# TensorE's order in two attention stages, laid out by the kernel itself

## The chip, the cores and the metric

The kernel runs on one core of a Trainium2 chip. The metric is the device time of one execution in microseconds (us). The kernel before took 3550.54 us, the median of three runs (3549.37 to 3552.87). A core has five engines that matter here, each with a queue of its own that it works through in order: TensorE (PE in the profile: matmuls and transposes), VectorE (DVE), ScalarE (ACT), GpSimd (POOL) and SyncE (SP), which here issues the DMAs. They wait for each other by semaphores.

## The reference

The program computes two layers of a hybrid block over 512 tokens of width 1024, and then one second block. Only two of the four branches of the second block change. Both are attention over 16 heads of 64, and both start from the normed input `h`:

```python
fq = _rms(_heads(proj("fox_q"), FOX_HEADS), fox_q_norm_g[l])
fk = _rms(_heads(proj("fox_k"), FOX_HEADS), fox_k_norm_g[l])
log_f = jax.nn.log_sigmoid(proj("fox_f") + b_forget[l])
# fox, per block of 128 queries
logits = einsum('bhqd,bhkd->bhqk', qi, k) * scale + (fi - cum_f)
p = softmax(where(k_pos <= q_pos, logits, -inf));  y = p @ v
# stick-breaking, per block of 128 queries
z = einsum('bhqd,bhkd->bhqk', qi, k) * scale
log_1m_beta = where(causal, log_sigmoid(-z), 0.0)
excl = cumsum(log_1m_beta, axis=3, reverse=True) - log_1m_beta
weights = where(causal, exp(log_sigmoid(z) + excl), 0.0);  y = weights @ v
# all four branches
gates = sigmoid(proj("gates") + b_gate[l])
mixed = sum(gates * einsum('bsnc,ncd->bsnd', branches, w_branch[l]), axis=2)
```

## The kernel before

All data stay transposed in SBUF, with features on the partitions and the 512 tokens along the free axis. A product in single precision is made of three matmuls with operands split into a high and a low part (`mm3`, L308 to L310: high by high, high by low, low by high). Weights come by DMA as `raw`; ScalarE makes the high part (L293), GpSimd or VectorE the low part (L296, in turns).

The second block runs its branches one behind the other: mem, fox, lru, sb (stick-breaking). In fox and sb the heads go in pairs p, since two heads of 64 fill the 128 partitions. The steps are

- `Q`p and `K`p: a projection of 24 matmuls of 128x512 into a bank `pd`. In fox the norm of K follows (`knorm`): sums by head on TensorE into the bank `pm`, a reciprocal root on GpSimd, a copy on VectorE (L860), a broadcast by four transposes (L864), a product on VectorE (L895). Then `halves` splits K on ScalarE (L427) and GpSimd (L429), and `stack_k` copies the halves by four DMAs of SP (L449) into the tiles `qk` and `e`. Q goes the same way by `stack_q` (L440).
- `V`g: values of four heads, 96 matmuls of 128x256 into `pd`.
- `H`h: one head. Four rows of logits (128 queries by 128, 256, 384 and 512 keys) by two matmuls each into `pa` (L456). In fox each row then gets its bias (made on GpSimd, L1014 and L1016), its minimum on VectorE (L473), the exponential on ScalarE, the reciprocal on VectorE (L479) and the normalisation on GpSimd (L480). In sb each row goes through two sigmoids on ScalarE (L495, L496), two selects on GpSimd (L498), a scan on VectorE (L501) and a multiply on GpSimd (L502). Then `weigh` transposes the weights by ten transposes into `pt` (L514), ScalarE and VectorE split them (L302, L303), eight matmuls sum the values into `po` (L523), and `fold` brings `po` out (VectorE, L532). The second head of a pair ends with `ys`, the pair's output, split by L302.
- `G`d: one of the eight gates of the branch, 24 matmuls into `pd`, a product on VectorE (L910) and a DMA to memory.

Behind the heads `branch` multiplies the `ys` with the branch's weights in the bank `pa`, 24 matmuls for each of eight tiles.

The kernel calls these steps in the order of two written plans, `FOX_PLAN` (L34) and `SB_PLAN` (L36), through `run` (L950). That is the program's order, not yet the engines' order: a scheduler at build time, with a timing model of its own, then chooses for every engine the order of its instructions, within the data's dependencies. In the trace heads, projections and gates therefore stand mixed. Banks bound what can overlap: two `pd`, two `pa` (three in sb, with `pm`), two `pt`, one `po`, one `pm`.

Of the kernel before, what the change touches and what calls it, by code (L numbers as in the profile page):

```python
# [10 lines left out]
def _warn_once_fixed(msg, *args, **kwargs):  # L11
# [6 lines left out]
FT = mybir.dt.float32  # L18
# [4 lines left out]
P = 128  # L23
# [173 lines left out]

class Build:
    def __init__(self, ctx, tc, I):
        self.tc, self.nc, self.I = tc, tc.nc, I  # L200
        nc = self.nc
# [104 lines left out]
    def mm3(self, out, wh, wl, xh, xl, start, stop):  # L306
        mm = self.nc.tensor.matmul
# [33 lines left out]
    def rstd_of(self, acc, d):  # L341
        nc = self.nc
        pt = self.ps("pm")
        for t in range(4):
            nc.tensor.matmul(pt[:, t:t + 1], acc[:, t * P:(t + 1) * P], self.ones[:, 0:1], start=True, stop=True)
# [3 lines left out]
        for t in range(4):  # L349
            nc.tensor.transpose(pt[:, t * P:(t + 1) * P], y[:, t:t + 1].to_broadcast([P, P]), self.ident)  # L350
# [102 lines left out]
    def dots(self, ps, q, k, s, t, n):  # L453

        for x in range(2):
            self.nc.tensor.matmul(ps[:, :n], q[:, s, t], k[s][:, x, :n], start=x == 0, stop=x == 1)  # L456

    def head(self, q, k, rows, bias, v, sub, y, tmp=None, scale=None):


        nc = self.nc
        st, po = self.sp.tile([P, 1280], FT, name="st"), self.ps("po")
        for i in range(4):
            n = (i + 1) * P
            c = slice(OFF[i], OFF[i] + n)
            ps = self.logits()
            t = slice(i * P, (i + 1) * P)
            if rows is None:
                self.dots(ps, q, k, sub, t, n)
            else:  # L470
                self.mm3(ps[:, :n], q[rows, 0, t], q[rows, 1, t], k[rows, 0, :n], k[rows, 1, :n], True, True)
            mn, sm = self.tiny(1, "ta"), self.tiny(1, "ta")
            nc.vector.tensor_tensor_reduce(st[:, c], ps[:, :n], bias(i), -1.0, 3e38, OP.add, OP.min, mn)  # L473
            f = -1.0
            if scale is not None:
                f = scale(i)
                nc.vector.tensor_scalar(mn, mn, f, -1.0, op0=OP.mult, op1=OP.mult)
            nc.scalar.activation(st[:, c], st[:, c], AF.Exp, bias=mn, scale=f, accum_out=sm)
            nc.vector.reciprocal(sm, sm)  # L479
            nc.gpsimd.tensor_scalar(st[:, c], st[:, c], sm, 0.0, op0=OP.mult, op1=OP.add)  # L480
        self.weigh(st, v, sub, po)
        self.fold(po, y, tmp)

    def stick(self, q, k, v, sub, y, tmp):

        nc = self.nc
        st, po = self.sp.tile([P, 1280], FT, name="st"), self.ps("po")
        for i in range(4):
            n = (i + 1) * P
            ps = self.logits()  # L490
            t = slice(i * P, (i + 1) * P)
            self.dots(ps, q, k, sub, t, n)
            r = self.f()
            o = OFF[i]
            nc.scalar.activation(r[:, :n], ps[:, :n], AF.Sigmoid, scale=-1.0)  # L495
            nc.scalar.activation(st[:, o:o + n], ps[:, :n], AF.Sigmoid)  # L496
            for d, fill in ((r[:, t], 1.0), (st[:, o + n - P:o + n], 0.0)):
                nc.gpsimd.affine_select(out=d, in_=d, pattern=[[-1, P]], compare_op=OP.is_gt, fill=fill, base=0,  # L498
                                        channel_multiplier=1)
            b = r[:, :n][:, ::-1]  # L500
            nc.vector.tensor_tensor_scan(b, b, b, 1.0, op0=OP.mult, op1=OP.min)  # L501
            nc.gpsimd.tensor_mul(st[:, o:o + n - 1], st[:, o:o + n - 1], r[:, 1:n])  # L502
        self.weigh(st, v, sub, po)
        self.fold(po, y, tmp)

    def weigh(self, st, v, sub, po):

        nc = self.nc
        va = v.rearrange("p a b -> p (a b)")
        for js in ((0,), (1,), (2, 3)):  # L510
            pt, at, cols = self.ps("pt"), 0, []
            for j in js:
                for i in range(j, 4):
                    nc.tensor.transpose(pt[:, at + (i - j) * P:at + (i - j + 1) * P],  # L514
                                        st[:, OFF[i] + j * P:OFF[i] + (j + 1) * P], self.ident)
                cols.append((j, at))
                at += S - j * P
            w = self.hl("pt")
            self.split(w, pt[:, :at], cols=slice(0, at))
            for j, c in cols:  # L520
                o = j * 256 + sub * P
                for x in range(2):
                    nc.tensor.matmul(po[:, j * P:], va[:, o:o + P], w[:, x, c:c + S - j * P], start=j == 0 and x == 0,  # L523
                                     stop=j == 3 and x == 1)
# [819 lines left out]
```

## Time and profile before

| | |
|---|---|
| median of three runs | 3550.54 us (3549.37 to 3552.87) |
| the profiled execution | 3547.29 us, span 3545.5 us, granted clock 0.99 |
| TensorE busy | 3450.4 us, 97% of the span, 16,392 instructions |
| VectorE, ScalarE, GpSimd busy | 55%, 40%, 43% |
| DMA | 397.57 MB, 112 GB/s |
| fox, 2350 to 2600 us | TensorE idle 13.9 us, of which 11.4 behind 2540 |
| sb, 2860 to 3106 us | TensorE idle 9.8 us, of which 4.6 behind 3060 |

Idle time of TensorE is the length of a window less the first number of busy time in its row. PEclk is the share of the full clock (2.4 GHz) that was granted to TensorE; at 0.5 it runs at 1.2 GHz. In a timeline a number in brackets is how long the engine stood idle ahead of the row, and behind it what released it.

### The profile page before, as it was taken

The numbers are of one execution on the slowest core, as the hardware profiler recorded it, in microseconds if no ns is written. First come the engines' busy times: TensorE is split into PE (matmuls) and PEld (weight loads), VectorE is DVE, ScalarE is ACT, GpSimd is POOL, SyncE is SP. The second block draws the span as 40 slices with busy tenths as digits, with TensorE's granted clock in tenths as the row PEclk, the third lists the DMA queues.
The fourth block names the chain that finished last, engine by engine and source line by source line (L and its number), as shares of the span: only waits on it lengthen the run. The fifth ranks groups of instructions, "written<-read, shape, count | busy, mean of one in ns | idle before, by whom it ended". The sixth has DMA issues, their size and how long they took to land.

```text
span 3545.5 us, 44868 instructions
## 1 busy us (share of the span) xinstructions
PE 3450.4 (97%) x16392; PEld 2864.3 (81%) x16392; DVE 1967.6 (55%) x3210; ACT 1435.7 (40%) x2366; POOL 1536.4 (43%) x1224
## 2 busy tenths in 40 slices
PE   8999999999999999999999999999999999999999
PEld 7888777788888888777888888888777788888887
DVE  5434697653445344796643456348646656657363
ACT  4223455532233223465432245346635445533222
POOL 3333346342424242446333344248545567635342
PEclk9999999999999999999999999999999999999999
DMA  4233433323233334334323233244532454442332
GB/s 135 92 104 106 129 94 110 115 95 95 99 97 96 93 98 130 109 91 118 117 90 109 85 124 119 97 137 141 151 122 89 164 154 137 120 143 96 95 101 89
DMA packets 141259, 397.57 MB, mean 112 GB/s; under 512 B 18144, under 2 KB 21600, under 8 KB 141040
## 3 DMA queue, kind: packets, MB, share of 16 engines
q1 hardware_dynamic: 141040, 394.71, 36.1%
q8 instruction: 130, 2.13, 0.2%
q14 instruction: 89, 0.73, 0.1%
HBM read 327.24 MB, written 20.48 MB: 98 GB/s over the span
## 4 chain that ended last, share of the span: by engine, by line
PE 47%; DVE 5%; ACT 2%; POOL 2%; issue 2%; DMA 1%; SPq 0%; POOLq 0%; DVEq 0%; ACTq 0%
PE pd L308 10%; PE pd L309 10%; PE pd L310 10%; PE pa L308 4%; PE pa L309 4%; PE pa L310 4%; PE po L523 1%; PE pt L514 1%; PE pa L456 1%; DVE wl L296 1%; DVE st L1083 0%; ACT wh L293 0%; POOL st L502 0%; DVE x L658 0%; DVE t L657 0%
## 5 line engine op out<-in xcount | busy, mean ns | idle before, releaser
L296 POOL TENSOR_TENSOR wl<-raw,wh 128x1024 fp32r<-128x1024 f32 (+3 forms) x315 | 719.6, 2285 | 1130.9 <-ACT wh L293 1122.2
L293 ACT ACTIVATE wh<-raw 128x1024 fp32r<-128x1024 f32 (+3 forms) x631 | 609.6, 967 | 1322.7 <-PE pd L309 841.9
L308 PE MATMUL pd<-hs,wh 128*128 128x512 f32 (+1 forms) x2008 | 792.4, 395 | 21.3 <-ACT wh L293 7.4
L310 PE MATMUL pd<-hs,wl 128*128 128x512 f32 (+1 forms) x2008 | 790.5, 394 | 2.9 <-DVE wl L296 1.7
L309 PE MATMUL pd<-hs,wh 128*128 128x512 f32 (+1 forms) x2008 | 789.4, 393 | 3.0 <-DVE hs L303 2.9
L296 DVE TENSOR_TENSOR wl<-raw,wh 128x1024 fp32r<-128x1024 f32 (+3 forms) x316 | 386.4, 1223 | 226.8 <-ACT wh L293 219.9
L308 PEld LDWEIGHTS pd<-hs,wh 128*128 128x128 f32 (+1 forms) x2008 | 378.1, 189 | 102.8 <-ACT wh L293 13.6
L310 PEld LDWEIGHTS pd<-hs,wl 128*128 128x128 f32 (+1 forms) x2008 | 378.2, 188 | 86.5 <-DVE wl L296 4.6
L309 PEld LDWEIGHTS pd<-hs,wh 128*128 128x128 f32 (+1 forms) x2008 | 378.5, 189 | 83.9 <-DVE hs L303 5.5
L308 PE MATMUL pa<-hs,wh 128*128 128x512 f32 x896 | 349.4, 390 | 0.0
L310 PE MATMUL pa<-hs,wl 128*128 128x512 f32 x896 | 349.0, 390 | 0.0
L309 PE MATMUL pa<-hs,wh 128*128 128x512 f32 x896 | 349.0, 390 | 0.0
L408 POOL TENSOR_TENSOR f<-f,g 128x512 f32<-128x512 f32 x88 | 145.7, 1658 | 280.3 <-ACT g L406 263.6
L407 DVE TENSOR_TENSOR f<-pa,rb 128x512 f32<-128x512 f32 x88 | 60.8, 691 | 272.4 <-PE pa L310 272.4
L309 PEld LDWEIGHTS pa<-hs,wh 128*128 128x128 f32 x896 | 168.4, 188 | 35.1
L308 PEld LDWEIGHTS pa<-hs,wh 128*128 128x128 f32 x896 | 168.3, 188 | 34.9
L310 PEld LDWEIGHTS pa<-hs,wl 128*128 128x128 f32 x896 | 168.2, 188 | 34.8
L480 POOL TENSOR_SCALAR st<-st,ta 128x128 f32<-128x128 f32 x192 | 109.4, 574 | 96.1 <-DVE ta L479 83.5
L308 PE MATMUL pd<-ys,wh 128*128 128x512 f32 x362 | 143.8, 397 | 1.7 <-DVE f L737 1.6
L309 PE MATMUL pd<-ys,wh 128*128 128x512 f32 x362 | 142.7, 394 | 0.0
L310 PE MATMUL pd<-ys,wl 128*128 128x512 f32 x362 | 142.6, 394 | 0.0
L303 DVE TENSOR_TENSOR pt<-pt 128x384 fp32r<-128x384 f32 (+1 forms) x200 | 115.8, 595 | 31.0 <-ACT pt L302 29.9
(385 smaller groups left out, 6441.2 us busy)
## 6 DMA issues: line engine op xcount, KB each, us to landing
raw<-in_wg_dram SPq DMA_DIRECT2D x88, 512.0 KB, 3.4
raw<-in_wu_dram SPq DMA_DIRECT2D x88, 512.0 KB, 3.4
raw<-in_win_dram SPq DMA_DIRECT2D x38, 512.0 KB, 3.5
qk<-nt SPq DMA_DIRECT2D x76, 256.0 KB, 3.9
raw<-in_w2gt_dram SPq DMA_DIRECT2D x32, 512.0 KB, 3.3
raw<-in_w2br_dram SPq DMA_DIRECT2D x32, 512.0 KB, 3.4
qk<-nt SPq DMA_DIRECT2D x108, 128.0 KB, 2.4
raw<-in_wd1a_dram SPq DMA_DIRECT2D x32, 384.0 KB, 3.1
```

The source lines that it names most:

```text
L293: nc.scalar.activation(h[:, :n], raw[:, :n], AF.Copy)
L296: (nc.vector if sub == "v" else nc.gpsimd).tensor_sub(lo[:, :n], raw[:, :n], h[:, :n].bitcast(FT))
L303: (eng or nc.vector).tensor_sub(dst[rows, 1, cols], src, dst[rows, 0, cols].bitcast(FT))
L308: mm(out, wh, xh, start=start, stop=False)
L309: mm(out, wh, xl, start=False, stop=False)
L310: mm(out, wl, xh, start=False, stop=stop)
L407: nc.vector.tensor_mul(u, pu, rb)
L408: nc.gpsimd.tensor_mul(ga, ga, s)
L456: self.nc.tensor.matmul(ps[:, :n], q[:, s, t], k[s][:, x, :n], start=x == 0, stop=x == 1)
L480: nc.gpsimd.tensor_scalar(st[:, c], st[:, c], sm, 0.0, op0=OP.mult, op1=OP.add)
L514: nc.tensor.transpose(pt[:, at + (i - j) * P:at + (i - j + 1) * P], st[:, OFF[i] + j * P:OFF[i] + (j + 1) * P], self.ident)
L523: nc.tensor.matmul(po[:, j * P:], va[:, o:o + P], w[:, x, c:c + S - j * P], start=j == 0 and x == 0, stop=j == 3 and x == 1)
```

## The change

The order of fox's and sb's matmuls and transposes is no longer left to the scheduler. While `drive` runs, each of them goes through `Pinned`, which ties it behind the TensorE instruction issued before it. The other engines, the DMAs and all other stages are ordered by the scheduler as before.

The order itself comes from `drive`. Every step is now a generator that issues a piece and yields. `drive` keeps a made-up clock, `now`, which moves on by the length of the matmuls issued (`step`), and by 0.2 us where nothing can be issued. Heads come first in the list, then the plan's projections and gates. A piece is issued when its bank is free and its delay has run out: a head's transposes 5.0 us behind its last dots (`soft`; in sb 7.0, `stick`), its weighted sums 2.5 us behind their transposes (`part`), a pair's dots 6.0 us behind Q's and K's end (`stack`), the sums of the norms 2.5 us behind the projection (`sum`), the broadcast 5.0 us behind the sums (`factor`), a bank's next use 2.0 us behind the last. The plans now hold all eight gates of each branch, and gates 5 to 7 wait until the last Q, K and V are issued. In fox before, two gates (6 and 7) were made inside `branch`.

```diff
-FOX_PLAN = ("F0 Q0 K0 V0 Q1 H0 K1 H1 Q2 H2 K2 H3 V1 Q3 H4 K3 H5 Q4 H6 K4 H7 V2 Q5 H8 K5 H9 G0 Q6 H10 K6 G1 H11 V3 Q7 "
-            "H12 G2 K7 H13 G3 H14 G4 H15 G5")
...
+FOX_PLAN = "F0 Q0 K0 V0 Q1 K1 Q2 K2 V1 Q3 K3 Q4 K4 V2 Q5 K5 Q6 K6 V3 Q7 K7 G0 G1 G2 G3 G4 G5 G6 G7"
+SB_PLAN = "Q0 K0 V0 Q1 K1 Q2 K2 V1 Q3 K3 Q4 K4 V2 Q5 K5 Q6 K6 V3 Q7 K7 G0 G1 G2 G3 G4 G5 G6 G7"
+DELAY = {"soft": 5.0, "stick": 7.0, "part": 2.5, "bank": 2.0, "stack": 6.0, "sum": 2.5, "factor": 5.0, "poll": 0.2}
...
+class Pinned:
+    def _keep(self, ins):
+        if self.on:
+            self.tc.keep_in_program_order(ins)
+        return ins
+    def matmul(self, *a, **k):
+        return self._keep(self.nc.tensor.matmul(*a, **k))
...
+def step(n):
+    return max(0.109, n / 2400 + 0.0135)
...
+    def knorm_g(self, ps, rb, gain, out):
+        nc = self.nc
+        f = self.f()
+        nc.vector.tensor_mul(f, ps, rb)
+        sq = self.square(None, f)
+        yield from self.until(self.now + DELAY["sum"])
+        b = yield from self.take("pm")
+        y = self.col_sum_rms(sq, self.bones, 64, 2)
+        self.now += 0.4
+        yield True
+        yield from self.until(self.now + DELAY["factor"])
+        pb = self.col_bcast(y, 2)
+        self.now += 1.1
+        nc.vector.scalar_tensor_tensor(f, pb, gain, f, op0=OP.mult, op1=OP.mult)
+        self.give("pm", b)
+        out.extend(self.stack_k(self.halves(f), tags=("qk", "e")))
+        yield True
...
+    def take(self, kind):
+        b = self.free[kind]
+        while min(b) > self.now:
+            yield
+        i = b.index(min(b))
+        b[i] = float("inf")
+        return i
...
+    def drive(self, plan, steps, heads, banks):
+        self.now, self.done = 0.0, {}
+        self.free = {k: [0.0] * n for k, n in banks.items()}
+        live = [(st, steps[st[0]](int(st[1:]))) for st in heads.split() + plan.split()]
+        self.te.on = True
+        while live:
+            for t in live:
+                try:
+                    if next(t[1]) is None:
+                        continue
+                except StopIteration:
+                    self.done[t[0]] = self.now
+                    live.remove(t)
+                break
+            else:
+                self.now += DELAY["poll"]
+        self.te.on = False
...
+    def stick_g(self, q, k, v, sub, y, tmp):
+        st = self.sp.tile([P, 1280], FT, name="st")
+        for i in range(4):
+            b = yield from self.take("pa")
+            self.stick_row(st, i, q, k, sub)
+            self.now += 2 * step((i + 1) * P)
+            self.give("pa", b)
+            yield True
+        yield from self.weigh_g(st, self.now + DELAY["stick"], v, sub, y, tmp)
+
+    def weigh_g(self, st, t, v, sub, y, tmp):
...
+        yield from turn((0,))
+        yield from turn((1,))
+        b = yield from self.take("po")
+        po = self.ps("po")
+        yield from weigh((0,))
+        yield from turn((2, 3))
+        yield from weigh((1,))
+        yield from weigh((2, 3))
+        self.fold(po, y, tmp)
+        self.give("po", b)
...
         def head(h):
             p, s = divmod(h, 2)
+            yield from self.after([f"Q{p}", f"K{p}"], DELAY["stack"])
+            yield from self.after([f"V{h // 4}", "F0"] + [f"H{h - 2}"] * (h > 1), DELAY["bank"])
...
+        def gate(d):
+            if d > 4:
+                yield from self.after(["Q7", "K7", "V3"])
+            yield from self.gate_g(0, d, hs, rb, "fa")
+
+        self.drive(FOX_PLAN, {"F": forget, "V": values, "Q": queries, "K": keys, "H": head, "G": gate},
+                   " ".join(f"H{h}" for h in range(16)), {"pd": 2, "pa": 2, "pt": 2, "po": 1, "pm": 1})
```

What moves shows best in three places. In the rows, the lines are those of each kernel's own program (the changed kernel's matmuls all stand at L211, its transposes at L214), and `x2` counts equal instructions in a row.

TensorE in fox, before: from the broadcast of K's norm of the seventh pair (`pm<-cst,fa`) to the pair's first dots (`pa<-qk 128x128`).

```order
L864 MATMUL pm<-cst,fa 128x128 x4
L308 MATMUL pd<-wh,hs 128x256
...
L523 MATMUL po<-pt,v 128x128 x2
L514 MATMUL pt<-cst,st 128x128 x3
L308 MATMUL pd<-hs,wh 128x512
...
L310 MATMUL pd<-hs,wl 128x512
L456 MATMUL pa<-qk 128x128 x2
L456 MATMUL pa<-qk 128x256 x2
```

The same place after:

```order
L214 MATMUL pm<-cst,fa 128x128 x4
L211 MATMUL pd<-hs,wh 128x512 x2
L211 MATMUL pd<-hs,wl 128x512
...
L211 MATMUL pd<-hs,wl 128x512
L211 MATMUL pa<-qk 128x128 x2
L211 MATMUL pa<-qk 128x256 x2
L214 MATMUL pm<-prm,g 128x2 x4
```

Before, 110 rows lie between the broadcast and the dots, with pieces of other heads among them; after, 27 matmuls of one projection.

GpSimd in sb, before: the end of the queue's work for the pair of heads 4 and 5 (`st_24591` is the first head, `st_24673` the second; `nt` are halves of a later Q or K, `wl` a weight's low part).

```order
L502 TENSOR_TENSOR st_24591<-st_24591,f_24632 128x511
L502 TENSOR_TENSOR st_24673<-st_24673,f_24678 128x127
L502 TENSOR_TENSOR st_24673<-st_24673,f_24690 128x255
L498 AFFINE_SELECT f_24702<-f_24702 128x128
L498 AFFINE_SELECT st_24673<-st_24673 128x128
L498 AFFINE_SELECT f_24714<-f_24714 128x128
L498 AFFINE_SELECT st_24673<-st_24673 128x128
L502 TENSOR_TENSOR st_24673<-st_24673,f_24702 128x383
L429 TENSOR_TENSOR nt_24791<-f_24789,nt_24791 128x512
L502 TENSOR_TENSOR st_24673<-st_24673,f_24714 128x511
```

The same place after (`st_24465` and `st_24502`):

```order
L530 TENSOR_TENSOR st_24465<-st_24465,f_24515 128x511
L530 TENSOR_TENSOR st_24502<-st_24502,f_24527 128x127
L321 TENSOR_TENSOR wl_24838<-raw_24836,wh_24837 128x1024
L530 TENSOR_TENSOR st_24502<-st_24502,f_24539 128x255
L454 TENSOR_TENSOR nt_24553<-f_24551,nt_24553 128x512
L526 AFFINE_SELECT f_24577<-f_24577 128x128
L526 AFFINE_SELECT st_24502<-st_24502 128x128
L526 AFFINE_SELECT f_24589<-f_24589 128x128
L526 AFFINE_SELECT st_24502<-st_24502 128x128
L454 TENSOR_TENSOR nt_24634<-f_24632,nt_24634 128x512
L530 TENSOR_TENSOR st_24502<-st_24502,f_24577 128x383
L530 TENSOR_TENSOR st_24502<-st_24502,f_24589 128x511
```

A weight's split and a second `nt` now stand between the two heads' last multiplies.

TensorE at the end of fox, before: the last head's weighted sums (`po<-pt,v`), then the branch (`pa<-ys`).

```order
L514 MATMUL pt<-cst,st 128x128 x3
L523 MATMUL po<-pt,v 128x512 x2
L523 MATMUL po<-pt,v 128x384 x2
L523 MATMUL po<-pt,v 128x256 x2
L523 MATMUL po<-pt,v 128x128 x2
L308 MATMUL pa<-ys,wh 128x512 x2
L309 MATMUL pa<-ys,wh 128x512
```

The same place after:

```order
L211 MATMUL po<-pt,v 128x256 x2
L211 MATMUL po<-pt,v 128x128 x2
L211 MATMUL pd<-hs,wh 128x512 x2
L211 MATMUL pd<-hs,wl 128x512
...
L211 MATMUL pd<-hs,wl 128x512
L211 MATMUL pa<-ys,wh 128x512 x2
L211 MATMUL pa<-ys,wl 128x512
```

Between the last weighted sum and the branch's matmuls that need the last `ys` there are now 39 matmuls of gates 6 and 7.

## Rows read from the trace of the kernel before

**Rows 1.** the page, part 1: busy us, share of the span, instructions of each engine

```profile
PE 3450.4 (97%) x16392; PEld 2864.3 (81%) x16392; DVE 1967.6 (55%) x3210; ACT 1435.7 (40%) x2366; POOL 1536.4 (43%) x1224
```

**Rows 2.** windows of fox and sb: PE, PEld, DVE, ACT, POOL busy, PEclk, DMA

```profile
2350.00:2540.00 190.00, 187.50 (x1145) 165.44 (x1143) 135.86 (x434) 114.26 (x240) 135.85 (x190) 1.00 0.52 149
2540.00:2600.00 60.00, 48.58 (x217) 38.09 (x215) 27.20 (x74) 28.46 (x49) 24.88 (x34) 0.86 0.29 89
2860.00:3060.00 200.00, 194.76 (x1123) 170.34 (x1122) 119.55 (x166) 108.02 (x231) 142.11 (x184) 1.00 0.47 129
3060.00:3106.00 46.00, 41.42 (x196) 33.98 (x195) 31.70 (x40) 25.35 (x48) 28.82 (x40) 0.93 0.37 114
```

**Rows 3.** windows inside the ends of the two stages

```profile
2559.00:2577.00 18.00, 11.90 (x36) 9.15 (x37) 8.79 (x36) 11.02 (x23) 8.94 (x20) 0.53 0.34 94
3098.00:3107.00 9.00, 6.93 (x25) 4.87 (x24) 5.77 (x8) 3.86 (x5) 3.41 (x2) 0.81 0.12 28
```

**Rows 4.** timeline of PE in fox's end: start us, us, instruction, [idle before <-releaser]

```profile
2560.46 1.19 PE L456 MATMUL pa<-qk 128*128 128x128 f32 x4 [3.33 <-DMA qk<-nt]
2570.43 1.01 PE L456 MATMUL pa<-e,qk 128*128 128x384 f32 x2 [3.80 <-DVE ta L473]
...
2591.51 0.73 PE L308 MATMUL pa<-ys,wh 128*128 128x512 f32 x2 [2.06 <-ACT ys L302]
2592.57 0.40 PE L310 MATMUL pa<-ys,wl 128*128 128x512 f32 x1
2592.80 0.40 PE L309 MATMUL pa<-ys,wh 128*128 128x512 f32 x1
```

**Rows 5.** timeline of PE in sb's end

```profile
3101.19 0.73 PE L308 MATMUL pa<-ys,wh 128*128 128x512 f32 x2 [2.06 <-ACT ys L302]
```

**Rows 6.** timeline of PE in fox's middle

```profile
2398.76 0.66 PE L864 MATMUL pm<-cst,fa 128*128 128x128 f32 x4 [1.33 <-DVE fa L860]
```

**Rows 7.** timeline of all engines, K's chain of two pairs in fox

```profile
2446.10 0.38 PE L864 MATMUL pm<-cst,fa 128*128 128x128 f32 x2
2447.40 0.72 DVE L895 SCALAR_TENSOR_TENSOR f<-pm,prm,f 128x512 f32<-128x512 f32 x1
2448.87 1.30 POOL L429 TENSOR_TENSOR nt<-f,nt 128x512 fp32r<-128x512 f32 x1
2450.19 1.11 SPq L449 DMA_DIRECT2D qk<-nt  x2
...
2553.11 0.74 DVE L895 SCALAR_TENSOR_TENSOR f<-pm,prm,f 128x512 f32<-128x512 f32 x1
2555.91 1.11 SPq L449 DMA_DIRECT2D qk<-nt  x2
```

**Rows 8.** GpSimd by form, 2860 to 3060: busy us, mean ns, idle; L498 min/median/max

```profile
L296 POOL TENSOR_TENSOR wl<-raw,wh 128x1024 fp32r<-128x1024 f32 x14 | 34.0, 2428 | 40.2 <-ACT wh L293 40.2
L498 POOL TENSOR_SCALAR_AFFINE_SELECT f<-f 128x128 f32<-128x128 f32 x53 | 27.1, 517 | 7.6 <-ACT f L495 7.6
L429 POOL TENSOR_TENSOR nt<-f,nt 128x512 fp32r<-128x512 f32 x14 | 21.8, 1559 | 4.8 <-ACT nt L427 4.8
L502 POOL TENSOR_TENSOR st<-st,f 128x511 f32<-128x511 f32 x12 | 16.5, 1376 | 6.9 <-DVE f L501 6.9
...
L498 POOL TENSOR_SCALAR_AFFINE_SELECT f<-f x53: 283/407/1214, 2876.5 to 3059.6; 128x128 f32<-128x128 f32 x53
```

**Rows 9.** timeline of one head of sb: its last dots, its last multiply

```profile
2946.28 0.64 PE L456 MATMUL pa<-e,qk 128*128 128x512 f32 x2
2954.37 2.08 POOL L502 TENSOR_TENSOR st<-st,f 128x511 f32<-128x511 f32 x1
```

**Rows 10.** GpSimd by form, fox, 2350 to 2540

```profile
L1014 POOL TENSOR_SCALAR x<-x,cq,iw 128x512 f32<-128x512 f32 x14 | 10.9, 777 | 1.0 <-DVE ta L473 1.0
L480 POOL TENSOR_SCALAR st<-st,ta 128x512 f32<-128x512 f32 x13 | 9.0, 695 | 2.4 <-DVE ta L479 1.3 <-DVE cq L879 1.0
```

**Rows 11.** waits of PE in sb: us in total, times, longest us

```profile
PE po L523 <- DVE x L532: 4.2, 4, 2.3
```

More of the change, by code (lines that the diff above doesn't have):

```diff
@@ L455, in dots @@
         for x in range(2):
-            self.nc.tensor.matmul(ps[:, :n], q[:, s, t], k[s][:, x, :n], start=x == 0, stop=x == 1)
+            self.te.matmul(ps[:, :n], q[:, s, t], k[s][:, x, :n], start=x == 0, stop=x == 1)
     def head(self, q, k, rows, bias, v, sub, y, tmp=None, scale=None):
-        nc = self.nc
         st, po = self.sp.tile([P, 1280], FT, name="st"), self.ps("po")
         for i in range(4):
[L464 to L480, printed above, removed]
@@ L481, in head, with soft @@
-        self.weigh(st, v, sub, po)
+            self.soft(st, i, q, k, rows, bias, sub, scale)
+        for js in ((0,), (1,), (2, 3)):
+            self.weighed(po, self.turned(st, js), v, sub)
         self.fold(po, y, tmp)
-    def stick(self, q, k, v, sub, y, tmp):
+    def soft(self, st, i, q, k, rows, bias, sub, scale):
         nc = self.nc
[L487 to L491, printed above, removed]
-            self.dots(ps, q, k, sub, t, n)
[L493 to L504, printed above, removed]
@@ L506, in weigh @@
-    def weigh(self, st, v, sub, po):
-        nc = self.nc
[L509 to L524, printed above, removed]
+        n = (i + 1) * P
@@ new lines, in soft @@
+        c = slice(OFF[i], OFF[i] + n)
+        ps = self.logits()
+        t = slice(i * P, (i + 1) * P)
+        if rows is None:
+            self.dots(ps, q, k, sub, t, n)
+        else:
+            self.mm3(ps[:, :n], q[rows, 0, t], q[rows, 1, t], k[rows, 0, :n], k[rows, 1, :n], True, True)
+        mn, sm = self.tiny(1, "ta"), self.tiny(1, "ta")
+        nc.vector.tensor_tensor_reduce(st[:, c], ps[:, :n], bias(i), -1.0, 3e38, OP.add, OP.min, mn)
+        f = -1.0
+        if scale is not None:
+            f = scale(i)
+            nc.vector.tensor_scalar(mn, mn, f, -1.0, op0=OP.mult, op1=OP.mult)
@@ new lines, in turned, with weighed @@
+    def turned(self, st, js):
+        pt, at = self.ps("pt"), 0
+        for j in js:
+            for i in range(j, 4):
+                self.te.transpose(pt[:, at + (i - j) * P:at + (i - j + 1) * P],
+                                  st[:, OFF[i] + j * P:OFF[i] + (j + 1) * P], self.ident)
+            at += S - j * P
+        w = self.hl("pt")
+        self.split(w, pt[:, :at], cols=slice(0, at))
+        return js, w
+    def weighed(self, po, jw, v, sub):
+        va, c = v.rearrange("p a b -> p (a b)"), 0
+        for j in jw[0]:
+            o = j * 256 + sub * P
+            for x in range(2):
+                self.te.matmul(po[:, j * P:], va[:, o:o + P], jw[1][:, x, c:c + S - j * P], start=j == 0 and x == 0,
+                               stop=j == 3 and x == 1)
+            c += S - j * P
@@ L624, in mix @@
         nc.vector.tensor_mul(f[0:96], f[0:96], tk[0:96])
[L625 removed]
+        self.te.matmul(pk, self.cst[:64, P:2 * P], f[:64], start=True, stop=True)
         ki = self.hl("pt")
@@ L948, in conv, with give, until, after @@
                                            op0=OP.mult, op1=OP.add)
+    def take(self, kind):
[5 more added lines that the diff above has]
+        return i
+    def give(self, kind, i, lag=None):
+        self.free[kind][i] = self.now + (DELAY["bank"] if lag is None else lag)
+    def until(self, t):
+        while self.now < t:
+            yield
+    def after(self, names, lag=0.0):
+        while not all(n in self.done and self.done[n] + lag <= self.now for n in names):
+            yield
@@ new lines, in proj_g, with tokens_g @@
+    def proj_g(self, out, w, hs, m=P):
+        wh, wl = w
+        n = len(hs)
+        for k, h in enumerate(hs):
+            c = slice(k * m, k * m + m)
+            self.mm3(out, wh[:, c], wl[:, c], h[:, 0, :], h[:, 1, :], k == 0, k == n - 1)
+            self.now += 3 * step(S)
+            yield True
+    def tokens_g(self, hs, ws, wn, kg, n, done, nt=4):
+        K = len(hs)
+        for t in range(nt):
+            b = yield from self.take("pd")
+            out = self.ps()
+            c = slice(t * P, (t + 1) * P)
+            for k in range(K):
+                wh, wl = ws[k // kg]
+                o = (k % kg) * wn
+                self.mm3(out[:, :n], hs[k][:, 0, c], hs[k][:, 1, c], wh[:, o:o + n], wl[:, o:o + n], k == 0, k == K - 1)
+                self.now += 3 * step(n)
+                if k < K - 1:
+                    yield True
+            done(t, out)
+            self.give("pd", b)
+            yield True
```

169 lines of the change are left out of this document (125 added, 44 removed).

## The prediction

> **What bounds the kernel now.** I read the page first: TensorE is busy 97% of the span, VectorE 55%, GpSimd 43%, ScalarE 40% [rows 1]. TensorE's idle time, not the load of another engine, is what a new order can win or lose. Then the windows of the two stages that change, fox (2350 to 2600 us) and stick-breaking, sb (2860 to 3106) [rows 2]. The reader is to see four numbers: TensorE stands idle 2.5 us in fox's middle (190.00 - 187.50), 11.4 in fox's end (60.00 - 48.58), 5.2 in sb's middle and 4.6 in sb's end: 23.7 us in all. Next the windows inside the two ends [rows 3]: from 2559 to 2577 the granted clock is 0.53, so nearly everything there ran at the lower of the two levels (1.2 instead of 2.4 GHz), and it is 0.81 from 3098 to 3107. A matmul of 512 columns starts every 0.23 us at the full level (2592.57 to 2592.80) [rows 4]. Busy time at half clock costs half of itself: 11.90 us busy at about 0.53 holds about 5.6 us lost; two stretches at the end of sb lose some 1.7 us each. So the clock costs another 9 us. TensorE's timeline of fox's end [rows 4] names the waits: 3.33 us for a DMA that brings K (qk<-nt), 3.80 us for a row's minimum, 2.06 us for the last head's output (ys) with nothing else left to do; sb's end has the same 2.06 us [rows 5]. A wait of 1.33 us earlier in fox [rows 6] left the clock at full.
>
> Behind the waits of 2.06, 3.33 and 3.80 us the clock fell. The Trainium skill ("TensorE: Matmul & The Clock Gate", What's actually happening) says that the throttled state is the default and that activity releases it; the trace agrees as far as 0.53 behind the two long waits goes [rows 3]. By that rule every new wait of this size would be paid nearly twice; by the 1.33 us row it would be paid once.
>
> **Part by part.** The instructions of TensorE are the same 16,248 before and after; only the order changes, in fox and sb alone. So the sum is waits removed against waits added, each in TensorE's time.
>
> *Removed: the two ends.* In before the last heads end directly ahead of the branch's matmuls. Now 39 matmuls of gates 6 and 7 (39 x 0.23 = 8.9 us) stand behind fox's last head, and 87 of gates (20 us) behind sb's; both cover a wait of 2.06 us. The gate weights' DMAs and GpSimd's splits move with them and lie in time that these engines have free (43%). If all of the end's idle time and clock goes: 11.4 + 5.6 in fox, 4.6 + 3.4 in sb = 25 us.
>
> *Removed: the middles.* The 2.5 + 5.2 us of waits belong to an order that no longer exists; I count all 7.7 as removed and the new order's waits below in full. Removed in all: 33 us.
>
> *Added: K's chain in fox.* After the broadcast of the key norm (the four 128x128 transposes into pm), VectorE multiplies, ScalarE and GpSimd make the halves, SP issues two DMAs, and only when these land may the pair's first row of logits start. In before the distance on TensorE was some 12 us. In the new order it is 6.1 us for the pair shown (27 matmuls of 0.227), and 6.0, 5.8, 6.6, 4.7, 6.1, 6.5, 6.1, 6.3 for the eight, mean 6.0. The trace prices the chain: VectorE starts at 2447.40, GpSimd ends at 2450.17, SP has issued at 2451.30 [rows 7]; in the pair for which TensorE really waited, VectorE started at 2553.11 and the dots at 2560.46 [rows 4, 7], 7.35 us, after a start that was already 2.8 us late. So a chain that meets no queue takes 7.4 us, one at the shortest that I found complete took 8.1, the mean of eight is 9.5. The shortfall per pair is 1.4, 2.1 or 3.5 us, times eight 11, 17 or 28 us. I take 17: the new order puts fewer pieces between one chain's steps on the other engines than before, so it should lie near the short ones. SP's queue holds weight loads beside these DMAs, and whatever waits behind them waits too.
>
> *Added: second heads late on GpSimd, sb.* A row of stick-breaking costs GpSimd two selects and a multiply. In the new GpSimd order the pair of heads 4 and 5 (st_24465, st_24502) has 16 selects, 8 multiplies, one weight split and two halves from first to last: by the means [rows 8] 16 x 0.517 = 8.3, 6.9 for the eight multiplies (up to 1.376 at 511 columns), 2.43 and 2 x 1.56, together 20.7 us; with the shortest select (283 ns) and the shortest of the others that I found, 16. TensorE's new order asks for the last of it 13.9 us after the first dots, so it waits 2 to 7 us. In before the same sum left slack, except at one head. Head by head with median durations the second heads of six pairs come late by 2.0, 3.5, 0.6, 3.5, 0.6 and 1.8 = 12 us. I take 12, with 3 (all at the shortest) and 20 (all at the mean) as ends. That this chain can be slow is in the row of a head whose last dots end at 2946.92 and whose last multiply ends at 2956.45 [rows 9], 9.5 us, where the new delay is 7.0.
>
> The selects spread from 283 over 407 to 1214 ns [rows 8]. The Trainium skill ("SBUF — State Buffer", Who interferes with whom) says that GpSimd and VectorE share one pair of ports as an exclusive lock. The trace agrees in that one form of instruction shows a factor of four. By that rule a denser order would make GpSimd's share longer than the medians and the wait near 7 us; by the shortest rows it would be 2.
>
> *Added: the same in fox.* There GpSimd makes the bias (0.777 us at 512 columns) [rows 10] and the normalisation of every row; by the same count four heads come late by 0.6, 1.3, 3.0 and 0.6: 5.5 us, I take 5, ends 0 and 10.
>
> *Added: K and Q in sb.* Three pairs have 6.1, 7.2 and 7.2 us from the projection's end to the dots. The shortest chain in the trace was 8.3, relaxed ones 11: 4.4 to 12 us. TensorE waits for GpSimd in the same pairs, and waits that overlap are paid once: I take 4, ends 0 and 12.
>
> *Added: splits and folds.* From transposes to the weighted sum the new order leaves 2.0 to 3.6 us; medians before were 2.2 to 2.9 in fox, 3.7 in sb. From one head's sum to the next it leaves 1.4 to 3.25 (fox) and 2.1 (sb), and the bank must first be folded: in sb this was already the largest wait, 4.2 us in four [rows 11]. I take 4, ends 0 and 10.
>
> *Added: the clock.* If half of the eight K waits reach 2 us, each followed by a stretch that loses 1.7 us, that is 6 us; ends 0 and 20.
>
> Edits without a price: the heads cut into generators issue the same instructions; the DMA of the cumulative forget sums moves ahead of four transposes at the start, where fox's first heads are far off.
>
> Sum: 17 + 12 + 5 + 4 + 4 + 6 = 48, less 4 for waits of one pair that overlap, 44, less the 33 removed: +11 us. The profiled execution took 3547.29 us, 3.25 under the median of 3550.54; against the median that is 3562 us.
>
> **Rivals.**
> *The queues follow (faster).* The other engines' order is laid anew around the pinned one, and each chain meets no queue: K's chain 11, sb's GpSimd 3, fox's 2, nothing else: 16 - 33 = -17, about 3533. For it: nothing but TensorE is over 55%. Against it: even without a queue 7.4 us don't fit into 6.0. It decides if K's chain stays under 7.5 us from broadcast to dots.
> *Traded evenly (no change).* K 17, GpSimd 9, the rest 6, no clock: 32 against 33, 3550.
> *The clock decides (much slower).* K's chain at its mean of 9.5 us gives eight waits of 3.5 us, and the low clock stands behind each: 28 + 12 + 5 + 4 + 20 - 33 = +36, 3587. For it: the two waits over 3 us in before were followed by 0.53 [rows 3].
> *It doesn't do what it says:* branch matmuls, which are not pinned, are put in between pinned ones and take the cover away at the ends, so that 10 of the 25 us stay on top of the sum: 3572.
>
> **How the numbers follow.** Less than 0.2%, or 7 us, can't be told from no change. My forecast (3558 to 3577) has 0.31, the even trade 0.20, the queues that follow 0.30, the clock 0.14, the last one 0.05. So slower 0.50, same 0.20, faster 0.30. The range takes the faster case at its centre and the clock case, 3530 to 3588; the forecast's own range is 3556 to 3576.
>
> **What would show it.** K's waits: TensorE idle in fox's pairs ahead of `pa<-qk`, released by the DMA qk<-nt, 1.4 us or more, about eight times. GpSimd: idle ahead of the transposes `pt<-cst,st` in sb, released by `st`, in six second heads. The ends: idle under 3 us in all. The clock: under 0.95 in slices of the middle of fox. I am wrong if the waits ahead of `pa<-qk` are few or under 1 us, or if the ends still wait.

## The result and the profile after

The changed kernel takes 3610.42 us (3608.84 to 3612.61), 1.0171 of before [1.0158, 1.0184]: 60 us slower, where 11.5 slower was forecast, and outside the range. The page's head and its first part:

```profile
span 3610.9 us, 44850 instructions
...
PE 3475.7 (96%) x16392; PEld 2882.3 (80%) x16392; DVE 1957.8 (54%) x3210; ACT 1442.5 (40%) x2368; POOL 1527.7 (42%) x1224
```

Against [rows 1] the span grew by 65.4 us. TensorE's busy time grew by 25.3 with the same 16,392 instructions; the other 40.1 us are idle time. The windows of fox and stick-breaking, to set beside [rows 2] (the busy times come in the order PE, PEld, DVE, ACT, POOL; then PEclk):

```profile
2310.00:2350.00 40.00, 38.70 (x230) 31.59 (x229) 17.10 (x44) 18.50 (x29) 16.58 (x16) 1.00 0.49 144
2350.00:2540.00 190.00, 171.35 (x1001) 149.03 (x1000) 111.07 (x377) 98.46 (x208) 111.87 (x165) 0.95 0.39 111
2540.00:2630.00 90.00, 81.96 (x383) 66.51 (x382) 42.87 (x124) 50.09 (x81) 43.48 (x55) 0.94 0.44 133
...
2888.00:3090.00 202.00, 171.80 (x969) 149.33 (x969) 115.29 (x159) 103.56 (x224) 130.77 (x182) 0.94 0.37 101
3090.00:3170.00 80.00, 74.67 (x343) 60.65 (x342) 36.79 (x44) 31.22 (x55) 40.55 (x42) 0.96 0.42 135
```

Idle in fox: 1.3 + 18.7 + 8.0 = 28.0 us (13.9 before); in sb: 30.2 + 5.3 = 35.5 (9.8 before). The difference, 39.8 us, is all but 0.3 of the idle time that came; the other stages don't matter. And the granted clock, 1.00 in both middles before, is 0.95 and 0.94. Counted as in the prediction, busy time times the share of the clock that is missing, the five windows lose some 27 us and those of [rows 2] some 10, so about 17 of the 25.3 us are the clock (an estimate). The rest need not be: a matmul of 512 columns is counted busy for 0.40 us and the next starts 0.23 behind it [rows 4], so every new wait also adds the end of the matmul ahead of it to the busy time. TensorE's waits by what ended them, in fox and then in sb (us in total, times, longest):

```profile
PE pa L211 <- issue: 7.6, 4, 2.9
PE pt L214 <- POOL st L512: 7.5, 7, 1.7
PE pd L211 <- DVE nt L456: 4.5, 4, 1.5
PE pa L211 <- DVE ta L505: 3.5, 4, 2.1
PE pa L211 <- DMA qk<-nt: 2.2, 2, 1.4
PE po L211 <- DVE pt L328: 1.3, 1, 1.3
PE pd L211 <- DVE fa L1069: 0.8, 1, 0.8
```

```profile
PE pt L214 <- POOL st L530: 17.1, 10, 3.4
PE pt L214 <- POOL f L526: 3.8, 2, 1.9
PE po L211 <- DVE pt L328: 2.8, 6, 1.0
PE pa L211 <- DMA qk<-nt: 2.6, 1, 2.6
PE pm L211 <- issue: 2.2, 1, 2.2
PE pd L211 <- DVE v L570: 1.9, 1, 1.9
PE pd L211 <- DVE f L1298: 1.7, 3, 0.7
PE pa L211 <- issue: 1.1, 1, 1.1
```

The reader should see three kinds here that the prediction had priced: dots that wait for K (`pa<-qk` and, in sb, `pm`, by "issue" and by DMA, 9.8 us in fox, 5.8 in sb), transposes that wait for GpSimd (7.5 in fox, 20.9 in sb), and weighted sums that wait for a split. Two kinds it had no term for: a projection that waits until its bank `pd` has been read (`nt`, `v`, `fa`, `f`), and dots that wait until a row minimum (`ta`) has read theirs. "Issue" says that the profile shows no releaser; that these are waits for K is read from the chain that follows.

One of the K waits, with its chain, answers to [rows 7]:

```profile
2476.87 0.60 PE L214 MATMUL pm<-cst,fa 128*128 128x128 f32 x4
...
2478.09 0.74 DVE L935 SCALAR_TENSOR_TENSOR f<-pm,prm,f 128x512 f32<-128x512 f32 x1
...
2480.29 1.28 POOL L454 TENSOR_TENSOR nt<-f,nt 128x512 fp32r<-128x512 f32 x1
...
2481.60 1.11 SPq L474 DMA_DIRECT2D qk<-nt  x2
...
2486.57 0.99 PE L211 MATMUL pa<-qk 128*128 128x128 f32 x4 [2.93 <-issue]
```

From the broadcast's end (2477.47) VectorE starts 0.6 us later, SP has issued by 2482.71, and the dots start at 2486.57, 9.1 us after the broadcast, having waited 2.93. It is the longest of the six such chains that TensorE waited for, which took 7.3 to 9.1, 8.2 in the mean, where the prediction's sum had 8.1. SP's issue came 5.2 us behind the broadcast's end, near the 4.8 of [rows 7]; the dots started 3.9 us after it, which is the page's median from issue to landing of these DMAs (3.9 us).

The pair of heads 4 and 5 of sb, whose GpSimd order stood ahead of the prediction, in the trace:

```profile
2965.70 2.40 POOL L321 TENSOR_TENSOR wl<-raw,wh 128x1024 fp32r<-128x1024 f32 x1
...
2968.06 0.64 POOL L530 TENSOR_TENSOR st<-st,f 128x255 f32<-128x255 f32 x1
...
2968.66 1.29 POOL L454 TENSOR_TENSOR nt<-f,nt 128x512 fp32r<-128x512 f32 x1
...
2969.90 1.28 POOL L526 TENSOR_SCALAR_AFFINE_SELECT f<-f 128x128 f32<-128x128 f32 x1
...
2971.14 0.29 POOL L526 TENSOR_SCALAR_AFFINE_SELECT st<-st 128x128 f32<-128x128 f32 x1
...
2972.55 1.26 POOL L454 TENSOR_TENSOR nt<-f,nt 128x512 fp32r<-128x512 f32 x1
...
2973.78 2.82 POOL L530 TENSOR_TENSOR st<-st,f 128x383 f32<-128x383 f32 x2
...
2975.60 0.48 PE L214 MATMUL pt<-cst,st 128*128 128x128 f32 x1 [3.40 <-POOL st L530]
```

It is the foreseen queue, instruction by instruction: the weight's split, the multiply of 255, a half, selects (of 1.28 and of 0.29 us), the second half, the last two multiplies. The transposes waited 1.91, 3.40 and 0.57 us, 5.9 in all, where 2 to 7 were worked out.

The clock, in windows around two short waits in fox, around one of 2.18 us in sb (`pm`, "issue") and around the waits of the pair above; then, in before, around fox's wait of 2.06 us for `ys` [rows 4]:

```profile
2377.00:2388.00 11.00, 8.70 (x34) 7.32 (x33) 4.08 (x19) 4.43 (x11) 7.30 (x10) 0.69 0.74 196
...
2953.00:2963.00 10.00, 7.82 (x40) 6.42 (x39) 6.55 (x8) 6.19 (x15) 6.44 (x14) 1.00 0.71 197
2969.00:2979.00 10.00, 4.12 (x19) 3.16 (x18) 6.58 (x7) 1.63 (x4) 7.59 (x8) 0.79 0.85 225
```

```profile
2589.00:2600.00 11.00, 8.61 (x39) 6.45 (x37) 4.50 (x6) 3.23 (x4) 5.88 (x3) 1.00 0.35 114
```

From 2377 to 2388 TensorE waits 1.53 us and, 0.7 us later, 0.77, and the granted clock is 0.69: a stretch at the lower of the two levels (1.2 GHz) follows, though neither wait is over 2 us. The lone wait of 2.18 us left the clock at full, as did in before those of 1.33 [rows 6] and 2.06. So in this kernel the length of a single wait does not tell whether the clock falls behind it.

### The profile page after: what moved, and what is told of

Read it like the earlier page. It is cut to its first block, busy times and chain, and to the rows that moved or that the text cites. A ratio compares the mean times of both kernels' runs of the same rounds, so it can differ in the third digit from the quotient of the medians.

```text
span 3610.9 us, 44850 instructions
## 1 busy us (share of the span) xinstructions
PE 3475.7 (96%) x16392; PEld 2882.3 (80%) x16392; DVE 1957.8 (54%) x3210; ACT 1442.5 (40%) x2368; POOL 1527.7 (42%) x1224
## 5 line engine op out<-in xcount | busy, mean ns | idle before, releaser
L211 PE MATMUL pd<-hs,wh 128*128 128x512 f32 x4016 | 1278.4, 397 | 29.9 <-ACT wh L318 7.4
L211 PEld LDWEIGHTS pd<-hs,wh 128*128 128x128 f32 x4016 | 753.3, 190 | 190.0 <-ACT wh L318 13.7
L211 PE MATMUL pd<-hs,wl 128*128 128x512 f32 (+1 forms) x2008 | 793.7, 395 | 2.9 <-DVE wl L321 1.7
L211 PE MATMUL pa<-hs,wh 128*128 128x512 f32 x1792 | 556.2, 390 | 0.0
L211 PEld LDWEIGHTS pd<-hs,wl 128*128 128x128 f32 (+1 forms) x2008 | 381.2, 190 | 90.0 <-DVE wl L321 4.6
L211 PEld LDWEIGHTS pa<-hs,wh 128*128 128x128 f32 x1792 | 336.4, 188 | 69.6
L211 PE MATMUL pa<-hs,wl 128*128 128x512 f32 x896 | 349.2, 390 | 0.0
L211 PE MATMUL pd<-ys,wh 128*128 128x512 f32 x724 | 227.6, 396 | 1.8 <-DVE f L765 1.6
L211 PEld LDWEIGHTS pa<-hs,wl 128*128 128x128 f32 x896 | 168.3, 188 | 35.0
L211 PE MATMUL pd<-wh,hs 128*128 128x256 f32 (+2 forms) x768 | 172.6, 306 | 0.0
L211 PE MATMUL pa<-ys,wh 128*128 128x512 f32 x512 | 159.9, 393 | 2.7 <-ACT ys L327 2.6
L211 PEld LDWEIGHTS pd<-ys,wh 128*128 128x128 f32 x724 | 136.8, 190 | 31.1 <-DVE f L765 2.4
L214 PE MATMUL pt<-cst,st 128*128 128x128 f32 x672 | 119.9, 287 | 35.2 <-POOL st L530 17.1
L327 ACT ACTIVATE pt<-pt 128x384 fp32r<-128x384 f32 (+1 forms) x200 | 100.6, 525 | 107.6 <-PE pt L214 106.1
L211 PE MATMUL pd<-ys,wl 128*128 128x512 f32 x362 | 142.5, 394 | 0.0
```

The source lines that it names most:

```text
L211: return self._keep(self.nc.tensor.matmul(*a, **k))
L214: return self._keep(self.nc.tensor.transpose(*a, **k))
L327: nc.scalar.activation(dst[rows, 0, cols], src, AF.Copy)
```

## Experiments

Excess, below, is the time between the starts of neighbouring TensorE instructions less the step at full clock (0.227 us for 512 columns, 0.12 for 256); it holds idle time and lost clock. "Before" was run beside every kernel; ratios are to it. All are edits of the changed kernel unless said otherwise.

**Each stage by itself.** Fox as changed, sb by the old plan (`run_g` runs each step to its end) and the scheduler's order.

```diff
-        self.drive(SB_PLAN, {"V": values, ...
+        self.run_g(SB_PLAN, {"V": values, ...
```

> Fox is laid out and kept as in the changed kernel; stick-breaking goes back to the old plan and the scheduler's order. Theory A (each stage loses by its own delays, which are shorter than the chains they stand for, and the clock falls behind the waits): fox keeps its loss of about 26 us (the stage's excess over full-speed steps was 51.8 us against 26.3), stick-breaking gives back about 37, so 3550 + 26 = 3576, between 3568 and 3584. Theory B (one cause outside the delays, such as the gates held back or the order of the other engines in the whole program): the loss is not split this way, below 3560 or above 3595.

3572.71 us, 1.0067 [1.0052, 1.0082]. Fox alone loses 24 us, as theory A has it; the 37 that are left for sb were not run alone.

**The same plans, nothing kept.**

```diff
-        self.te.on = True
+        self.te.on = False
```

> The same generators, plans and delays, but nothing is kept: the scheduler orders TensorE again. Theory A (the kept order asks for results before they are there): the scheduler puts other work there, and the time returns to the neighbourhood of before, 3540 to 3560. Theory B (the plan is at fault, heads first and gates held back, whoever orders TensorE): it stays above 3590.

3548.19 us, 0.9998 [0.9988, 1.0008]: no difference from before. Its windows of the two stages:

```profile
2310.00:2600.00 290.00, 280.99 (x1627) 240.64 (x1626) 184.70 (x545) 161.86 (x317) 178.92 (x234) 0.99 0.47 136
2860.00:3106.00 246.00, 231.19 (x1273) 199.13 (x1272) 150.74 (x199) 127.33 (x267) 171.71 (x216) 0.98 0.44 127
```

9.0 us idle in fox and 14.8 in sb, together 23.8 as in before. Fox stands idle 5 us less than before and sb 5 more; on balance plans, generators and gates cost nothing, and the order that is kept costs everything.

**One delay in sb.**

```diff
-DELAY = {"soft": 5.0, "stick": 7.0, ...
+DELAY = {"soft": 5.0, "stick": 9.0, ...
```

> Only the delay ahead of a stick-breaking head's transposes is raised, from 7.0 to 9.0 us; fox is as in the changed kernel. Theory A: the waits of the transposes for GpSimd's results, 20.9 us in this stage, shrink by up to 2 us each in about eight second heads, and the clock follows: 15 to 20 us less than the changed kernel's 3610, so 3590 to 3595. Theory C (GpSimd's throughput in this stage is the limit, whatever the delay): the waits only move, 3604 to 3612.

3590.60 us, 1.0119 [1.0104, 1.0134]: 20 us less (18 by the ratios), as theory A said. The transposes' waits for GpSimd fell from 20.9 to 5.1 us.

**One delay in fox and sb.** `"stack"` from 6.0 to 9.0.

> Only the delay between K's end and the pair's first dots is raised, from 6.0 to 9.0 us. Theory A: the waits for K, 9.8 us in fox and 5.8 in stick-breaking, go, with some of the clock: 15 to 22 us less than 3610, so 3588 to 3595. Theory D (chains that come one behind the other in a pair share their waits, so that what one gives back the next takes): above 3600.

3617.33 us, 1.0197 [1.0183, 1.0211]: not a gain, 9 us more by the ratios, though its four times are spread from 3612.63 to 3623.59. Theory A is wrong here, D is right. The waits for K are gone, but in fox:

```profile
PE pa L211 <- DVE ta L505: 18.3, 10, 7.4
PE pt L214 <- POOL st L512: 9.2, 6, 3.6
```

The row minimum, which cost 3.5 us in the changed kernel, now holds the second heads' dots for 18.3.

**All short delays.** `stack` 9, `stick` 10, `soft` 6.5, and in fox's `queries`:

```diff
-            self.give("pd", b)
+            self.give("pd", b, 4.0)
```

> All delays that were short are set by the waits measured in the changed kernel: K to dots 9.0 us, stick-breaking's transposes 10.0, fox's 6.5, and the bank of fox's Q projection held 4.0 us instead of 2.0. Theory A: waits for K (15.6 us), for GpSimd ahead of transposes (28.4) and for Q's bank (4.5) go almost wholly and two thirds of the clock's 35 us with the ends covered: 3535 to 3560. Theory C (a kept order has a floor: with two heads in flight the chains are longer than the work that can stand between them): 3575 to 3595.

3592.92 us, 1.0127 [1.0113, 1.0141]: theory C. Waits moved again; one of 3.96 us in fox, with what led to it, from the timeline of all engines:

```profile
2489.53 2.40 POOL L321 TENSOR_TENSOR wl<-raw,wh 128x1024 fp32r<-128x1024 f32 x1
...
2491.89 1.64 POOL L382 TENSOR_TENSOR tiny<-tiny 128x8 f32<-128x8 f32 x1
...
2493.52 0.77 POOL L1205 TENSOR_SCALAR x<-x,cq,iw 128x512 f32<-128x512 f32 x1
...
2496.04 0.55 POOL L1207 TENSOR_SCALAR_AFFINE_SELECT x<-x 128x128 f32<-128x128 f32 x2
2496.37 0.69 DVE L505 CUSTOM_DVE_ANT_0 st<-pa,x 128x512 f32<-128x512 f32 x1 [0.27 <-POOL x L1207]
...
2497.13 0.50 PE L211 MATMUL pa<-e,qk 128*128 128x256 f32 x2 [3.96 <-DVE ta L505]
```

A bias of 512 columns (`x`, at 2493.52) stands on GpSimd behind a weight's split of 2.40 us and a power of 1.64, and its select (at 2496.04) behind other rows' work; the minimum on VectorE waits for it, the bank `pa` for the minimum, and the second head's dots for the bank. VectorE stood idle for the select only 0.27 us, so its own queue was late too. The table counts that bank free 2.0 us behind the dots.

**GpSimd without weights.** In both stages VectorE makes every weight's low part (`vec` is set while they are laid out).

```diff
         hi, sub = WENG[self.wc % len(WENG)]
         self.wc += 1
+        if self.vec:
+            sub = "v"
```

> The changed kernel, but in fox and stick-breaking VectorE makes the low part of every weight (1.22 us each) instead of taking turns with GpSimd (2.4 us each, some 25 of them). Theory E (GpSimd works in order, and a weight's split standing ahead of a head's rows is what makes them late): the waits ahead of the transposes, 28 us in both stages, shrink to under 12, and with the clock the time falls by 20 to 30: 3580 to 3590. Theory F (fixed delays with two heads in flight are too short for the chains, whatever GpSimd holds): under 8 us less, 3602 to 3612.

3595.25 us, 1.0136 [1.0119, 1.0153]: 12 us less by the ratios, between the two theories. The waits for `st` fall from 7.5 to 3.7 us in fox and go in sb, but there 17.6 us for splits by VectorE (`pt`), 3.6 in the changed kernel, take their place:

```profile
PE po L211 <- DVE pt L331: 9.8, 6, 3.0
PE pt L214 <- DVE pt L331: 7.8, 2, 3.9
```

On top of the lengthened delays:

> The same on top of the lengthened delays (3593). There fox's second heads wait 21 us for the bank of their logits, because the row minimum waits for a bias that GpSimd makes behind a weight's split and a power (rows of that trace). Theory E: these waits halve and the clock follows, 3565 to 3578. Theory F: 3586 to 3595.

3579.57 us, 1.0093 [1.0078, 1.0108], 12 us less again and again between the theories; the waits for the minimum only went from 21.4 to 17.2 us. With K's halves on VectorE too:

> On top of the lengthened delays and the weights' low parts, VectorE also makes the low half of K (and of stick-breaking's Q), 1.3 to 1.56 us each on GpSimd. Theory E: a little better again than the run with the weights alone, by 3 to 8 us. Theory F, or VectorE now the late one: no gain or slower.

3582.03 us, 1.0096 [1.0081, 1.0111]: no gain. Taking the weights off GpSimd is worth some 12 us, net of what VectorE's new work costs; taking off more gave nothing. GpSimd's own wait for fox's row minimum, with the longer delays and here:

```profile
POOL x L1205 <- DVE ta L505: 37.9, 13, 8.0
```

```profile
POOL x L1210 <- DVE ta L508: 106.9, 12, 16.9
```

The less GpSimd has to do, the longer it stands idle until a minimum lets it begin the next bias, while TensorE's waits for the minimum (12.6 us here) stay the largest in fox. Fox's biases go through two tiles in turn (`rings["bt"][i % 2]`, in both kernels), so a bias can't be made before the minimum two rows ahead has read the tile. More such tiles were not tried.

**Work that nobody needs.** To part the clock from the waits, ahead of the first transposes of heads 1, 5, 9 and 13 of sb:

```diff
         pt, at = self.ps("pt"), 0
+        if junk is not None:
+            va = junk.rearrange("p a b -> p (a b)")
+            for x in range(14):
+                self.te.matmul(pt[:, :S], va[:, :P], va[:, :S], start=True, stop=True)
```

> The changed kernel with work added that nobody needs: 14 matmuls of 128x512 (3.2 us) ahead of the transposes of four second heads of stick-breaking, the ones with the longest waits for GpSimd (4.6, 5.9, 5.9 and 2.6 us), 12.7 us in all, into the bank that the transposes then overwrite. If the clock is a cost of its own that waiting brings on, the added work hides in 12.1 us of the waits and the clock of the stage comes back by 4 to 9 us: 3602 to 3607 against 3610 of the changed kernel. If the clock loss comes from elsewhere, 3610 to 3614.

3598.11 us, 1.0149 [1.0133, 1.0164]: with 12.7 us of work more, the kernel is 8 us faster by the ratios (12 by the medians), just clear of the noise. In the profiled execution TensorE's idle time is 13.2 us shorter than in the changed kernel's, about what was put in, and its busy time, which holds the added work, is 2.3 us shorter as well:

```profile
PE 3473.4 (97%) x16448; PEld 2878.3 (80%) x16448; DVE 1959.8 (55%) x3210; ACT 1443.0 (40%) x2368; POOL 1528.6 (43%) x1224
```

So it isn't the waits alone that pay: some 15 us came back in the work itself. The control, the same in heads 2, 6, 10 and 14:

> The control to the added work: the same 14 matmuls in four heads, but in first heads of pairs (2, 6, 10, 14), whose transposes hardly wait. If the added work paid before because it stood in place of waits and kept the clock up, it now costs all or most of its 12.7 us: 3617 to 3626 against the changed kernel's 3610. If any more work in this stage raises the clock, it is paid back here too: 3596 to 3606.

3618.36 us, 1.0185 [1.0171, 1.0199], 5 us slower than the changed kernel by the ratios (8 by the medians), which alone is within the noise, and 13 slower than the added work at the waits, which is not. The window 2887 to 3155 of the changed kernel, of the added work at the waits, and of the control:

```profile
2887.00:3155.00 268.00, 232.48 (x1253) 198.58 (x1252) 147.62 (x200) 132.01 (x276) 165.43 (x221) 0.94 0.38 109
```

```profile
2887.00:3155.00 268.00, 244.63 (x1337) 207.88 (x1336) 151.75 (x202) 132.85 (x275) 170.99 (x223) 0.99 0.39 115
```

```profile
2887.00:3155.00 268.00, 239.61 (x1275) 204.65 (x1274) 146.96 (x197) 130.80 (x272) 167.55 (x221) 0.94 0.37 108
```

The granted clock is 0.94, 0.99 and 0.94. At the waits the work brings the clock back; elsewhere it does not, though idle time falls there too (35.5 to 28.4 us). So the clock is a cost of its own that the waits bring on.

**The ends.** The order kept only from K7 on:

```diff
-        self.te.on = True
         while live:
+            self.te.on = "K7" in self.done
```

> The order is kept only from the end of the last K projection's chain on, so that the middles are the scheduler's and the ends have gates as cover behind the last heads. Theory A: the middles cost what they cost before, and the ends, 25 us of idle time and clock before, are mostly covered: 3525 to 3540. Theory B: above 3580, as the plan is still the new one.

3559.45 us, 1.0029 [1.0017, 1.0041]: a miss, 20 us above the expectation and 10 above before. Of what was kept, the heads in sb waited 3.9 us for GpSimd and those in fox some 2.6 for several engines. Waits as large, 3.8 us for a minimum in fox and 2.7 for GpSimd in sb, stand ahead of the kept part, at pieces that `drive` issues before K7 is done and the scheduler ordered. Which of it makes the 10 us was not settled.

**The best of both.** Fox by the new plan but nothing kept, sb by the old one:

> Fox by the new generators and plan but ordered by the scheduler, stick-breaking by its old plan. In the fully unpinned kernel fox's excess over full-speed steps was 18.4 us against 26.3 before, and stick-breaking's 24.0 against 18.3. If the stages add up, this is 8 us under before: 3541 to 3545. If the new plan has no merit of its own and that was chance of the scheduler, 3548 to 3553.

3542.62 us, 0.9982 [0.9973, 0.9991], where it should be if the stages add up. Fox's order here is that of the run with nothing kept, so whether the new plan has merit or this one order of the scheduler is lucky stays open. With the weights' low parts on VectorE:

> The same on top of fox unpinned with the old stick-breaking (3542.6). TensorE's idle time in both stages there is 23.5 us, of which GpSimd is named for 2 only, so theory E gives 0 to 5 us less: 3537 to 3543; if VectorE becomes late with 25 more splits, 3545 to 3555.

3536.12 us, 0.9967 [0.9954, 0.9980]: 0.3% faster than before, and the fastest of all; nothing in it is kept. Its windows:

```profile
2310.00:2600.00 290.00, 281.55 (x1616) 241.89 (x1614) 182.91 (x558) 159.54 (x314) 148.11 (x218) 0.97 0.45 134
...
2860.00:3100.00 240.00, 233.64 (x1305) 202.48 (x1304) 165.01 (x216) 131.83 (x277) 152.72 (x210) 0.99 0.45 129
```

8.5 and 6.4 us idle. And with only the matmuls of gates 6 and 7 kept at their place in the plan. In fox nearly all of them stand behind the last head; in sb, whose old plan calls gate 6 between heads 14 and 15, only gate 7 does:

```diff
-        yield from self.proj_g(pg, w, hs)
+        on, self.te.on = self.te.on, d > 5
+        for x in self.proj_g(pg, w, hs):
+            self.te.on = False
+            yield x
+            self.te.on = d > 5
+        self.te.on = on
```

> The best kernel so far (3536) with only the matmuls of gates 6 and 7 kept behind the last heads, in both stages; heads and all else stay with the scheduler. Theory A: the two waits of 2.06 us for the last output and the clock behind them go, and nothing is tied to a result that isn't there yet: 3528 to 3534. Theory G (matmuls held back for the end are missed as filler in the last pairs before it): 3536 to 3545.

3547.01 us, 0.9989 [0.9980, 0.9998]: 0.2% slower than without it, just above theory G's range. The waits for the last output (2.1 us twice) are gone, but fox's last dots wait 3.0 us for a minimum, and in the last pairs of sb stands

```profile
PE po L212 <- DVE pt L332: 4.4, 2, 4.3
```

of which one wait of 4.3; neither wait is in the run without it. That the matmuls saved for the end are missing as filler just before it, as theory G has it, fits these waits but was not tried by itself.

## Why the prediction was wrong

*The sign was right, and so were most of the places.* All in all 11 us were forecast and 60 came.

*The clock is the largest step that failed.* The prediction put 6 us for new clock loss and removed 9: a gain of 3. By the granted clock it came as a loss of some 17 us, 20 off (28 if all of the 25.3 us by which TensorE's busy time grew is set against it). The step that failed was "half of the eight K waits reach 2 us": it hung the clock on K's waits alone and on the length of each, and took the wait of 1.33 us that left the clock at full as a sign that shorter waits are paid once. In the trace waits of 1.53 and 0.77 us close together had a clock of 0.69, the waits of the pair shown in sb had 0.79, and added work in their place gave it back (0.94 to 0.99). The prediction also says that the clock fell behind the waits of 2.06 us; fox's did not do that (1.00 from 2589 to 2600), as its own row of matmuls 0.23 us apart right behind that wait shows [rows 4]. The rival in which the clock decides had the mechanism, with 0.14 for it; it hung it on K alone.

The Trainium skill ("TensorE: Matmul & The Clock Gate", What's actually happening) says that the clock is throttled by default and released by activity; the prediction weighed it as a rule by which every wait of about 2 us or more is paid nearly twice. Here 39.8 us of idle time came with 25.3 of busy time, 1.6 times in all and 1.4 by the clock alone: between that rule and the row that I followed.

*GpSimd in sb:* 12 us forecast, 20.9 came, at six second heads in the order that was worked out: 4.6, 5.9, 1.0, 5.9, 1.0 and 2.6 us for 2.0, 3.5, 0.6, 3.5, 0.6 and 1.8. The count by means was nearer than the one by medians that I summed: 20.7 us of work against 13.9 make 6.8 for the pair shown, and 5.9 came. (Half of the sixteen selects write `st`, whose mean in the same view was 438 ns and not 517; with it the count is 20.1 and 6.2.)

*Banks:* no term; 12.4 us came (fox 4.5 for `nt`, 3.5 for `ta`, 0.8 for a gate; sb 1.9 and 1.7). I priced the delays of the table that stand for chains and, of "bank", which stands for the reading of a bank, only the fold of `po`, though [rows 4] had a wait for `ta` of 3.80 us as its largest.

*K in fox:* 17 forecast, 9.8 came. The chain was as long as foreseen (8.2 us in the mean), but it made six waits of up to 2.9 us, not eight of 2.1: other waits and the lower clock between broadcast and dots took up part of it, and in two pairs all. *Fox's GpSimd* (5, came 7.5), *sb's K* (4, came 5.8) and *splits and folds* (4 in the two stages, came some 7) were near.

*The ends:* 25 us removed by count. Behind 2540 fox still has 8.0 us idle (11.4 before), sb's end 5.3 (4.6 before), where under 3 in all was forecast, and at clocks of 0.94 and 0.96 most of the lost clock is there as well. (These windows are longer than those of before, and their waits are counted above by kind.) The cover for `ys` did its work, but the last heads' own chains stayed, and in the two runs with only an end kept such cover was no gain.

*That waits overlap* was put at 4 us. The longer delays show how far it goes: K's waits taken away (15.6 us) gave back nothing, since in fox the next chain of the same pair took their place.

*A number that changes nothing:* the 16,248 instructions of TensorE are 16,392 on both pages.

*What is shown and what is not.* That the kept order, and not the plans, is the loss is shown (1.0171 against 0.9998); that the clock's part hangs on the waits is shown, for sb. The weights' splits on GpSimd are worth some 12 us. Why some 33 us stay with longer delays and GpSimd relieved (1.0093) was not settled: there the waits name the row minimum in fox and the reading of Q's and K's bank in sb. Whether a table with a longer time for these banks would do, or more than two tiles for the bias, was not tried.

## What to carry to other kernels

An order laid out by fixed delays is only as good as its shortest entry: count for every wait, banks included, what stands in the queue of the engine that ends it, with means rather than medians. Price idle time of TensorE together with the clock behind it, and price waits that lie close together as one, since here two of 1.53 and 0.77 us cost the clock that a lone one of 2.18 did not. A longer delay can move a wait instead of removing it (`stick` gave 18 us, `stack` none). Before keeping an order, run the same plan without keeping it: here that cost one line and showed where the loss was.

## What was not expected of the hardware

12.7 us of matmuls that compute nothing made the kernel some 8 us faster, by a granted clock of 0.99 instead of 0.94 over 268 us. A select of 128x128 on GpSimd took 1.28 us in the queue shown above and the next one 0.29, and it is this spread that makes the mean the better price. What lengthens a select, the ports shared with VectorE or something else, no run shows.
